# A quarter of the weights' low parts computed on GpSimd instead of VectorE, in one stage of a two-block network

## The chip, the cores and the metric

The kernel runs on one core of one Trainium2 chip. The metric is the device time of one execution in microseconds (us). The kernel before took 2920.99 us (median of 3 runs, 2920.43 to 2922.79).

## The reference

Two residual blocks are applied to one sequence of 256 tokens with 2048 channels, all in fp32. The first block mixes a gated linear recurrence, an attention with forget gates and a pooling branch, and ends with a feed-forward layer. The second block, in which the change lies, is:

```python
h = rms_norm_2(x, attn_norm_w[l])
proj = h @ w_cat
p_rwkv = proj[..., :N_RWKV_IN]
p_gdn = proj[..., N_RWKV_IN:N_IN]
...
y_a, v_first = rwkv7_mixer(p_rwkv, ...)
y_b = gdn_mixer(p_gdn, ...)
y = jnp.concatenate([y_a, y_b], axis=-1).astype(x.dtype)
x = x + y @ w_out[l]
h = rms_norm_2(x, ffn_norm_w[l])
x = x + (jax.nn.silu(h @ ffn_w_gate[l]) * (h @ ffn_w_up[l])) @ ffn_w_down[l]
```

`rwkv7_mixer` shifts each projection by one token, then runs a recurrence over 16 heads of 64 channels. `gdn_mixer` runs a causal convolution of width 4 over tokens, then a gated delta rule over 8 heads of 128 channels.

## The kernel before

Channels lie on the 128 partitions, tokens on the free axis (S = 256). Every large product is `out[128, 256] = sum over k of W_k^T x_k`, with weight tiles of 128 x 128. fp32 accuracy is kept with a split: `weights` (L302) loads a **piece** of up to eight weight tiles (128 x 1024) into `raw` by a DMA of SP's queue, ScalarE (`self.A`) rounds it to `hi` (L314) and VectorE (`self.V`) computes the low part `lo = raw - hi` (L315, by the helper at L206). The activations are split in the same way and stand as 512 columns, 256 high and 256 low. `step3` then issues two matmuls for each k: `hi` against the 512 columns, `lo` against the first 256. `product` (L319) is the loop over the pieces; a product of 2048 rows has two pieces, that is 32 matmuls. `raw` has four buffers, `hi` and `lo` three each. A result in PSUM is completed by `join` (ScalarE copies one half, VectorE adds the other) and `scaled` (a multiply on VectorE).

The stage that the change touches is `mixers` (L898): 51 products of `w2` in four groups, each with an RWKV part (`rwkv_front`, two slots of three products) and a GDN part (`gdn_front`, six products), and `out2_first`, 16 products of `wo2` with 12 tiles (a piece of eight and a piece of four). Between the products stands much small work: `shifted` (L959) and `gdn_front` (L1270) write the scaled projection into a tile whose first columns are zeroed; `rwkv_rest` (L1005) builds decays and chunk matrices `ab`; `diagonals` sends the 16 x 16 diagonal blocks of `ab` through DRAM (`scr`, `d`), inverts them in a chain of 30 small VectorE instructions (`etmp`, `e`), and sends the result back through DRAM (`scs`, `cmp`); `merged_inverse` builds from `cmp` the inverse of the whole chunk, level by level: transposes on TensorE, a copy to `xn` on ScalarE, matmuls with the masked part `off`, a step to `m`, matmuls, an update of `xt` on VectorE, and again. For a GDN group one such inverse serves the group, for an RWKV group there are two.

The order of the instructions on each engine is made by the scheduler of the Tile layer from priorities (`tc.high_priority`, with `ahead_mix = (139, 145)` for the weights in this stage) and from its own costs of the instructions; each engine then runs its list in order and waits on semaphores. `self.parted` marks the stage; the zero columns are written by GpSimd (`self.G.memset` at L962, L1011, L1280), which has no other work in this stage but one more memset.

Of the kernel before, what the change touches and what calls it, by code (L numbers as in the profile page):

```python
# [7 lines left out]
F32 = mybir.dt.float32  # L8
# [7 lines left out]
P = 128  # L16
# [166 lines left out]
class Prog:  # L183
# [83 lines left out]
    pieces = (4, 4, 4, 4)  # L267
    early = []
    parted = False
    narrow = nar3 = nar4 = False  # L270
    nar1 = nar2 = nar5 = True
    turn = 0
# [29 lines left out]
    def weights(self, src, nkt):  # L302

        parts = []
        ahead = self.ahead_mix if self.parted else (self.ahead[self.narrow],) * 2
        for k in range(0, nkt, 8):
            n = min(8, nkt - k) * P
            with self.tc.high_priority(offset=ahead[0]):
                raw = self.rawp.tile([P, n], F32, name="raw", tag="raw")
                self.nc.sync.dma_start(out=raw, in_=src[:, k * P:k * P + n])  # L310
            with self.tc.high_priority(offset=ahead[1]):
                hi = self.hip.tile([P, n], F32R, name="hi", tag="hi")
                lo = self.lop.tile([P, n], F32R, name="lo", tag="lo")
                self.A.copy(hi, raw)  # L314
                self.sub(lo, raw, hi.bitcast(F32))  # L315
            parts.append((k, n // P, hi, lo))
        return parts

# [476 lines left out]
class Block2(Block1):  # L795
# [25 lines left out]
    def block2(self):  # L821
        rh = lambda k, h=self.h: h[:, k]
        with ExitStack() as st:
            self.yp = self.pool("y2", 1, st=st)
            self.y = self.moving(self.yp, 8, "y", at=self.AT["y"])
            self.yg = [None] * 8
            with ExitStack() as st2:
                self.mixers(rh, st2)
            xst = ExitStack()
            self.x = self.pool("xres", 1, st=xst, side="right").tile([P, KT, S], F32, name="xres", tag="xres")  # L830
            self.narrow = self.nar5
            self.out2_second()
        self.narrow = False
        with xst:
            self.ffn("wg2", "wd2", 1e-5, self.feed_out, "left")
            self.last_norm()
# [61 lines left out]
    def mixers(self, rh, st):  # L898
        w2 = self.a["w2"]
        self.tp = self.pool("mx", 3, st=st)  # L900
        self.kp = kp = self.pool("mxk", 1, st=st)
        self.gp = self.pool("mxg", 1, st=st)
        self.parted = True
        self.narrow = self.nar3
        ps = self.product([(w2[0], KT)], rh)
        self.norm2_end()
        self.omu = kp.tile([P, 27], F32, name="omu")
        self.ts(self.omu, self.p("mu_rkv", 0, 27), -1.0, 1.0, ALU.mult, ALU.add)
        self.nka = kp.tile([P, 8], F32, name="nka")
        self.ts(self.nka, self.p("k_a", 0, 8), -1.0)  # L910
        self.wa = kp.tile([P, S], F32, name="wa")
        self.shifted(ps, self.wa, 24)
        self.act(self.wa[:64], self.wa[:64], AF.Tanh)
        self.gd = kp.tile([P, S], F32, name="gd")
        self.shifted(self.product([(w2[1], KT)], rh), self.gd, 25)
        self.mx = kp.tile([P, S], F32, name="mxt")
        self.shifted(self.product([(w2[2], KT)], rh), self.mx, 26)
        self.act(self.gd, self.gd, AF.Sigmoid)
        self.act(self.mx[64:], self.mx[64:], AF.Sigmoid)
        self.sigmoids()  # L920
        self.gdn_gates()
        pend = []
        for g in range(4):
            slots = self.rwkv_group(g, rh, w2)
            front = [self.rwkv_front(2 * g + j, j, rh, w2, slots) for j in range(2)]
            self.step(pend)
            pend.append((slots, front, g, True))
            self.step(pend, first=True)
            slots = self.gdn_group(g)
            front = [self.gdn_front(g, rh, w2, slots)]  # L930
            self.step(pend)
            pend.append((slots, front, g, False))
            self.step(pend, first=True)
        self.narrow = self.nar4
        self.out2_first()
        self.step(pend)
# [22 lines left out]
    def shifted(self, ps, o, j):  # L959

        t = self.w(S + 1, "shf")
        self.G.memset(t[:, 0:1], 0.0)  # L962
        self.scaled(ps, t[:, 1:])
        self.act(o, t[:, 1:], AF.Copy, scale=self.omu[:, j:j + 1])
        self.stt(o, t[:, :S], self.p("mu_rkv", j), o, ALU.mult, ALU.add)
# [39 lines left out]
    def rwkv_rest(self, j, slot, t, slots):  # L1005
# [2 lines left out]

        ch = lambda z: z.rearrange("p (c t) -> p c t", c=2)
        cw, e1, e2 = (ch(self.w(2 * (P + 1), n)) for n in ("cw", "e1", "e2"))  # L1010
        self.G.memset(cw[:, :, 0:1], 0.0)  # L1011
        for c in range(2):
            x = sg[:, c * P:(c + 1) * P]
            self.V.tensor_tensor_scan(out=cw[:, c, 1:], data0=self.c("ones"), data1=x, initial=0.0, op0=ALU.mult, op1=ALU.add)
# [52 lines left out]
        m = self.c("atmask")  # L1067
# [202 lines left out]
    def gdn_front(self, i, rh, w2, slots):  # L1270
        gp = self.gp

        big = gp.tile([P, 6, S], F32, name="gbig", tag="gbig")
        for b in range(6):
            ps = self.product([(w2[27 + 6 * i + b], KT)], rh)
            if b >= 4:
                self.scaled(ps, big[:, b])
                continue
            t = self.w(S + 3, f"gc{b}")
            self.G.memset(t[:, :3], 0.0)  # L1280
            self.scaled(ps, t[:, 3:])
            ch = (i, 4 + i, 8 + 2 * i, 9 + 2 * i)[b]
            o = big[:, b]
            self.act(o, t[:, :S], AF.Copy, scale=self.p("gconv", ch))
            for k in range(1, 4):
                self.stt(o, t[:, k:k + S], self.p("gconv", 16 * k + ch), o, ALU.mult, ALU.add)
        with self.tc.high_priority(offset=self.front_ahead):
            return self.gdn_rest(i, big, slots)
# [147 lines left out]
```

## Time and profile before

| | |
|---|---|
| median of 3 runs | 2920.99 us |
| the profiled execution: its own time / its span | 2924.65 us / 2922.9 us |
| TensorE matmul busy (PE) | 2888.2 us, 99% |
| TensorE weight load (PEld) | 2540.8 us, 87% |
| VectorE (DVE) | 1990.9 us, 68% |
| ScalarE (ACT) | 1506.3 us, 52% |
| GpSimd (POOL) | 21.5 us, 1%, 88 instructions |
| DMA | 515.78 MB, mean 176 GB/s |

Busy time is the union of an engine's instructions, the span is from the first to the last instruction. Matmuls are pipelined, so a busy PE need not be at its peak. The mixers and `out2_first` together lie at about 1571 to 2147 us of the span.

### The profile page before, as it was taken

The page shows a single profiled execution, that of the slowest core. Times are in us where ns is not written, and L with a number is a line of the kernel's source. Part 1 is how long each engine was busy: PE and PEld are TensorE (multiplying, and loading weights), DVE is VectorE, ACT ScalarE, POOL GpSimd, SP SyncE. Part 2 cuts the span into 40 slices and gives each one's busy share as a digit, 9 for nine tenths or more (in the row PEclk, how much of TensorE's full clock was granted, in tenths as well). Part 3 has the DMA queues.
Part 4 walks back from the last instruction along what each step waited for, and adds up shares of the span by engine and source line. Part 5 has one row for each costly group of instructions (what it writes and reads, how often), then busy time and mean ns, then how long its engine had stood idle before and what let it go on. Part 6 is the DMA issues. An engine that isn't in the chain of part 4 may idle for free. (4 is left out here: it accounts for less than half of the span.)

```text
span 2922.9 us, 46401 instructions
## 1 busy us (share of the span) xinstructions
PE 2888.2 (99%) x17676; PEld 2540.8 (87%) x17676; DVE 1990.9 (68%) x3393; ACT 1506.3 (52%) x2448; POOL 21.5 (1%) x88
## 2 busy tenths in 40 slices
PE   8999999999999999999999999999999999999998
PEld 8999988888888888888888878887888888888887
DVE  7855766666766665666667878888776665566665
ACT  6644454444554444444556555666564444444454
POOL 0000000000000000000000000000010000000000
PEclk9999999999999999999999999999999999999999
DMA  6544555555655556555565423233465555655554
GB/s 232 183 160 154 173 188 191 190 188 189 231 190 189 189 177 192 201 191 191 180 206 186 148 87 122 92 130 110 145 207 189 190 186 182 201 191 190 184 177 159
DMA packets 178047, 515.78 MB, mean 176 GB/s; under 512 B 32024, under 2 KB 59040, under 8 KB 177568
## 3 DMA queue, kind: packets, MB, share of 16 engines
q1 hardware_dynamic: 177536, 511.80, 51.9%
q8 instruction: 138, 2.26, 0.3%
q10 hardware_dynamic: 288, 1.02, 0.1%
q14 instruction: 85, 0.70, 0.1%
HBM read 505.66 MB, written 7.09 MB: 175 GB/s over the span
## 5 line engine op out<-in xcount | busy, mean ns | idle before, releaser
L233 PE MATMUL ps<-h,hi 128*128 128x512 f32 (+1 forms) x5904 | 1801.0, 366 | 1.2 <-DVE xp L206 0.9
L206 DVE TENSOR_TENSOR lo<-raw,hi 128x1024 fp32r<-128x1024 f32 (+2 forms) x1028 | 1156.6, 1125 | 759.0 <-ACT hi L314 754.9
L314 ACT CAST hi<-raw 128x1024 fp32r<-128x1024 f32 (+2 forms) x1028 | 997.2, 971 | 1193.3 <-issue 663.8
L233 PE MATMUL ps<-h,lo 128*128 128x256 f32 x5152 | 1410.6, 282 | 0.9 <-DVE lo L206 0.6
L233 PEld LDWEIGHTS ps<-h,hi 128*128 128x128 f32 x5904 | 1041.6, 188 | 164.4 <-issue 6.0
L233 PEld LDWEIGHTS ps<-h,lo 128*128 128x128 f32 x5152 | 969.5, 188 | 29.4 <-issue 2.4
L233 PE MATMUL ps<-mid,hi 128*128 128x512 f32 (+1 forms) x1452 | 486.2, 385 | 0.0
L233 PE MATMUL ps<-mid,lo 128*128 128x256 f32 x1408 | 386.1, 281 | 0.0
L233 PEld LDWEIGHTS ps<-mid,hi 128*128 128x128 f32 x1452 | 265.4, 188 | 50.5
L233 PEld LDWEIGHTS ps<-mid,lo 128*128 128x128 f32 x1408 | 265.1, 188 | 5.3
L206 DVE TENSOR_TENSOR t<-ps,s 128x256 f32<-128x256 f32 x323 | 134.8, 417 | 0.0
L381 ACT COPY s<-ps 128x256 f32<-128x256 f32 x323 | 118.3, 367 | 0.0
L233 PE MATMUL ps<-merged,hi 128*128 128x512 f32 x256 | 88.0, 392 | 0.0
L233 PE MATMUL ps<-merged,lo 128*128 128x256 f32 x256 | 69.0, 280 | 0.0
L233 PEld LDWEIGHTS ps<-merged,hi 128*128 128x128 f32 x256 | 47.0, 188 | 9.6 <-DVE merged L206 0.2
L233 PE MATMUL ps<-y,hi 128*128 128x512 f32 (+1 forms) x160 | 49.3, 359 | 1.7 <-ACT hi L314 1.4
L233 PEld LDWEIGHTS ps<-merged,lo 128*128 128x128 f32 x256 | 48.1, 188 | 1.3
L233 PE MATMUL ps<-yg,hi 128*128 128x512 f32 (+1 forms) x160 | 48.6, 354 | 0.0
L233 PE MATMUL ps<-yb,hi 128*128 128x512 f32 x128 | 46.1, 393 | 0.0
L233 PE MATMUL ps<-yc,hi 128*128 128x512 f32 x128 | 46.1, 393 | 0.0
L233 PE MATMUL ps<-ya,hi 128*128 128x512 f32 x128 | 45.9, 391 | 0.0
L206 DVE TENSOR_TENSOR t<-ps,xres 128x256 f32<-128x256 f32 x78 | 33.1, 424 | 12.9 <-PE ps L233 7.0
(383 smaller groups left out, 2307.8 us busy)
## 6 DMA issues: line engine op xcount, KB each, us to landing
raw<-wg SPq DMA_DIRECT2D x352, 512.0 KB, 4.2
raw<-w SPq DMA_DIRECT2D x292, 512.0 KB, 3.6
raw<-wd SPq DMA_DIRECT2D x128, 512.0 KB, 3.5
raw<-wbr SPq DMA_DIRECT2D x48, 512.0 KB, 3.5
raw<-wo SPq DMA_DIRECT2D x48, 512.0 KB, 4.3
raw<-wd SPq DMA_DIRECT2D x128, 192.0 KB, 3.1
raw<-wo SPq DMA_DIRECT2D x32, 256.0 KB, 3.2
xin<-x SPq DMA_DIRECT2D x4, 512.0 KB, 6.4
```

What stands on the lines that cost most here:

```text
L206: return (e or self.V).tensor_tensor(out=o, in0=x, in1=y, op=op)
L233: return self.T.matmul(o, lhsT=l, rhs=r, start=start, stop=stop, skip_group_check=True)
L314: self.A.copy(hi, raw)
L381: self.A.copy(s[:rows], ps[:rows, S:])
```

## The change

In the stage, a piece of more than 512 columns has its `lo` computed in two parts: VectorE takes the first three quarters (768 of 1024 columns), GpSimd the last quarter (256 columns). A flag `shared` is set where `parted` is set and cleared ahead of the last feed-forward layer. The pieces of 512 columns in `out2_first` and `out2_second` stay whole. The memsets of the zero columns in `shifted`, `rwkv_rest` and `gdn_front` move from GpSimd to VectorE.

```diff
@@ class Prog
+    shared = False
...
@@ weights
                 self.A.copy(hi, raw)
-                self.sub(lo, raw, hi.bitcast(F32))
+                m = n - 2 * P if self.shared and n > 4 * P else n
+                self.sub(lo[:, :m], raw[:, :m], hi[:, :m].bitcast(F32))
+                if m < n:
+                    self.sub(lo[:, m:], raw[:, m:], hi[:, m:].bitcast(F32), self.G)
...
@@ block2
-        self.narrow = False
+        self.narrow = self.shared = False
...
@@ mixers
-        self.parted = True
+        self.parted = self.shared = True
...
@@ shifted
-        self.G.memset(t[:, 0:1], 0.0)
+        self.V.memset(t[:, 0:1], 0.0)
...
@@ rwkv_rest
-        self.G.memset(cw[:, :, 0:1], 0.0)
+        self.V.memset(cw[:, :, 0:1], 0.0)
...
@@ gdn_front
-            self.G.memset(t[:, :3], 0.0)
+            self.V.memset(t[:, :3], 0.0)
```

The scheduler makes a new order for the whole stage. Line numbers of the changed kernel are larger by 1 to 4.

**Order 1.** GpSimd's whole list from the pooling branch on (`pu`, `gtr` are memsets that stay). First the first rows of it before, which go on in the same pattern, then all of it now:

```order
L682 MEMSET pu 128x2x16
L962 MEMSET shf 128x1 x6
L1011 MEMSET cw 128x2
L962 MEMSET shf 128x1 x3
L1011 MEMSET cw 128x2
L1280 MEMSET gc_16870 128x3
L1280 MEMSET gc_16926 128x3
```

```order
L1250 MEMSET gtr 128x256
L686 MEMSET pu 128x2x16
L206 ISA
L206 TENSOR_TENSOR lo<-raw,hi 128x256 x118
L206 TENSOR_TENSOR acc_22557<-acc_22557,q 128x256 x15
```

The 51 memsets of the stage are gone from GpSimd's list, and 118 subtractions stand in it: 102 pieces of the 51 products and the 16 pieces of eight tiles in `out2_first`. The 15 instructions on `acc` are those of `out2_second`, there before and after.

**Order 2.** SP's queue at the first RWKV group's way through DRAM (`raw` is a weight piece, `scs` the inverted diagonals going out, `cmp` the same coming back), before and now:

```order
L310 DMA raw<-w 128x1024
L1107 DMA d<-scr_16775 64x256
L310 DMA raw<-w 128x1024 x4
L1122 DMA scs_16819<-e 64x256
L310 DMA raw<-w 128x1024
L1124 DMA cmp<-scs_16819 128x8x16
L310 DMA raw<-w 128x1024 x3
```

```order
L311 DMA raw<-w 128x1024
L1111 DMA d<-scr_16793 64x256
L311 DMA raw<-w 128x1024 x5
L1126 DMA scs_16837<-e 64x256
L1128 DMA cmp<-scs_16837 128x8x16
L311 DMA raw<-w 128x1024 x3
```

Ahead of `scs` as many pieces are loaded as before (one fewer stands further up), and no piece is loaded any more between `scs` and `cmp`.

**Order 3.** TensorE's list at the inverse of the second GDN group, from its first transposes (`pb<-cst,xt`) on, before and now (`ps` rows are the large products, `pf` rows belong to the front of the next RWKV slot, `pb` rows to the inverse):

```order
L236 MATMUL pb<-cst,xt 128x128 x4
L233 MATMUL ps<-h,hi 128x512
L233 MATMUL ps<-h,lo 128x256
L233 MATMUL ps<-h,hi 128x512
L233 MATMUL ps<-h,lo 128x256
L233 MATMUL ps<-h,hi 128x512
L233 MATMUL pb<-xn,off 128x128 x4
L233 MATMUL ps<-h,lo 128x256
L233 MATMUL ps<-h,hi 128x512
L233 MATMUL pf<-tok,ak 128x64
```

```order
L236 MATMUL pb<-cst,xt 128x128 x4
L236 MATMUL pf<-cst,bt 128x128
L236 MATMUL pf<-cst,kt 128x128
L236 MATMUL pf<-cst,r_18910 128x128 x2
L233 MATMUL pf<-ar_19110,bt 128x256
L233 MATMUL pb<-xn,off 128x128 x4
L233 MATMUL pf<-ar_19110,bt 128x256
L233 MATMUL pf<-ar_19110,kt 128x256
L233 MATMUL pb<-xt,m_19456 128x128 x4
L233 MATMUL pf<-ar_19110,kt 128x256
L233 MATMUL pf<-ar_19111,bt 128x256 x2
L1167 MATMUL pb<-cst,xt 128x128 x4
```

Before, the steps of the inverse stood among large products: 13 of their matmuls from the first transposes to the second, 16 from there to the third. Now none stands there up to the second and 3 up to the third; work of the RWKV front lies between instead. The third GDN group's inverse has the same pattern, with 13 and 16 before and 4 and none now.

## Rows read from the trace of the kernel before

**Rows 1.** The page's first line.
```profile
span 2922.9 us, 46401 instructions
```
**Rows 2.** Stretches: us; busy (instructions) of PE, PEld, DVE, ACT, POOL; PEclk, DMA, GB/s.
```profile
1571.00:2147.00 576.00, 566.16 (x3524) 469.59 (x3523) 451.38 (x1103) 345.34 (x684) 5.25 (x48) 1.00 0.38 124
1780.00:1800.00 20.00, 20.00 (x117) 17.60 (x116) 18.05 (x51) 11.34 (x14) 0.00 (x0) 1.00 0.56 191
2020.00:2040.00 20.00, 20.00 (x117) 17.58 (x117) 18.56 (x55) 10.76 (x14) 0.00 (x0) 1.00 0.48 156
1684.00:1688.00 4.00, 1.73 (x7) 1.64 (x8) 2.48 (x5) 0.97 (x3) 0.00 (x0) 0.74 0.32 117
1688.00:1692.00 4.00, 4.00 (x28) 3.67 (x26) 2.65 (x6) 0.59 (x3) 0.10 (x1) 0.83 0.38 131
```
**Rows 3.** TensorE's longest waits, 1571 to 2147: us in total, times, longest.
```profile
PE pb L236 <- DVE xt L206: 3.5, 4, 2.8
PE ps L233 <- DVE lo L206: 1.7, 1, 1.7
```
**Rows 4.** VectorE's groups by shape, 1571 to 2147: busy us, mean ns | idle before.
```profile
L206 DVE TENSOR_TENSOR lo<-raw,hi 128x1024 fp32r<-128x1024 f32 x112 | 136.5, 1220 | 33.3 <-ACT hi L314 33.1
L206 DVE TENSOR_TENSOR lo<-raw,hi 128x512 fp32r<-128x512 f32 x21 | 14.4, 687 | 6.3 <-ACT hi L314 5.5 <-PE ps L233 0.3
...
L1016 DVE COPY mid<-cw 128x2 f32<-128x2 f32 x8 | 1.3, 164 | 0.1
```
**Rows 5.** GpSimd's largest group of memsets in the stage, same columns.
```profile
L962 POOL MEMSET shf<- 128x1 f32 x27 | 2.8, 110 | 1550.9 <-PE pf L233 1096.2 <-PE ps L233 424.3 <-DVE rs_w L206 14.2
```
**Rows 6.** Tile view of acc, GpSimd, 2140 to 2180: ns min/median/max.
```profile
L206 POOL TENSOR_TENSOR acc<-acc,q x15: 728/860/1685, 2147.6 to 2176.9; 128x256 f32<-128x256 f32 x15
```
**Rows 7.** Tile view of h, VectorE, 1400 to 1570, with GpSimd idle: same columns.
```profile
L218 DVE SCALAR_TENSOR_TENSOR h<-xres,gfa,h x16: 476/479/480, 1445.7 to 1563.8; 128x256 fp32r<-128x256 f32 x16
```
**Rows 8.** VectorE's groups by shape, 2145 to 2177, while GpSimd works on acc.
```profile
L218 DVE SCALAR_TENSOR_TENSOR h<-xres,par,h 128x256 fp32r<-128x256 f32 x15 | 10.5, 710 | 0.1
L206 DVE TENSOR_TENSOR lo<-raw,hi 128x512 fp32r<-128x512 f32 x13 | 9.7, 742 | 3.0 <-ACT hi L314 2.7
```
**Rows 9.** Timeline, 2157 to 2163: start, us, engine, instruction.
```profile
2160.22 1.89 POOL L206 TENSOR_TENSOR acc<-acc,q 128x256 f32<-128x256 f32 x2 [0.49 <-ACT q L230]
2160.26 1.24 DVE L206 TENSOR_TENSOR lo<-raw,hi 128x512 fp32r<-128x512 f32 x1
...
2161.43 0.96 DVE L218 SCALAR_TENSOR_TENSOR h<-xres,par,h 128x256 fp32r<-128x256 f32 x1
```
**Rows 10.** Timeline, 1677 to 1687: the first RWKV group's way through DRAM.
```profile
1677.47 0.47 SPq L1122 DMA_DIRECT2D scs<-e  x1
...
1678.61 0.33 SPq L310 DMA_DIRECT2D raw<-w  x1
...
1679.41 0.38 SPq L1124 DMA_DIRECT2D cmp<-scs  x1
...
1685.52 1.29 DVE L206 TENSOR_TENSOR xt<-cmp,cst 128x512 f32<-128x512 f32 x2 [3.08 <-DMA cmp<-scs]
...
1686.27 1.11 PE L236 MATMUL pb<-cst,xt 128*128 128x128 f32 x4 [2.84 <-DVE xt L206]
```
**Rows 11.** Tile view of cmp: from issue to landing, eight transfers.
```profile
DMA to landing us min/median/max: 1.8/2.4/6.1
```
**Rows 12.** Timeline, 1856 to 1863: the second GDN group's inverse, first level.
```profile
1856.36 0.66 PE L236 MATMUL pb<-cst,xt 128*128 128x128 f32 x4 [0.22 <-DVE xt L206]
...
1857.18 0.56 ACT L1139 COPY xn<-pb 128x512 f32<-128x512 f32 x1
...
1857.80 1.16 PE L233 MATMUL pb<-xn,off 128*128 128x128 f32 x8
...
1861.08 0.69 DVE L206 TENSOR_TENSOR xt<-pb,xt 128x512 f32<-128x512 f32 x1 [0.37 <-PE pb L233]
...
1862.42 0.60 PE L1163 MATMUL pb<-cst,xt 128*128 128x128 f32 x4
```

## The prediction

> **What bounds the kernel now.** I read the page first, then the stretch of the mixers by windows, then TensorE's waits in it, and last the timeline at the places where it waits. The profiled execution took 2924.65 us, with a span of 2922.9 [rows 1]; it lies 3.7 us above the median of the runs, 2920.99. The sum below is a difference within the profiled execution, and I add it to the median.
>
> In the stage that changes, 1571 to 2147, TensorE is busy for 566.16 of 576 us [rows 2]. What it stands idle there, 9.84 us, is nearly all that any edit of the other engines can win. To this comes some time at the lower clock: in 1684 to 1692 the granted clock was on average 0.74 and then 0.83 of the upper of its two levels (2.4 GHz; the lower is 1.2) [rows 2], right behind TensorE's longest wait [rows 3], and that costs 4 x 0.26 + 4 x 0.17 = 1.7 us. So the ceiling of a gain is 11.5 us, 0.4%. VectorE is busy for 451.38 us, 78%, but unevenly: where the six products of a GDN front follow each other TensorE runs without a gap, 117 matmuls in 20 us or 0.171 us each, and VectorE is at 18.05 to 18.56 of 20 us [rows 2]. For `lo` TensorE waited once, 1.7 us; its largest wait is for `xt`, the start of an inverse [rows 3]. A quicker `lo` as such thus frees little.
>
> The 0.2% by which I part faster from slower is 5.8 us, about what a measurement of this kernel tells from no change.
>
> **The subtraction on VectorE.** A `lo` of 1024 columns takes 1.220 us, one of 512 columns 0.687 [rows 4]. For 768 I take the middle, 0.954. The 118 pieces save 118 x 0.266 = 31.4 us of VectorE's time.
>
> **The subtraction on GpSimd.** The only two-input work of GpSimd in the trace, on 128x256 as here, took 728 ns at the least, 860 in the median, 1685 at the most [rows 6]. Its result is needed late: it holds the seventh and eighth weight tile, and TensorE has six pairs of matmuls before, 12 x 0.171 = 2.05 us. So TensorE waits for it only if it comes over 2 us behind VectorE's part, and I cost that at nothing; its cover is the lead of three `lo` buffers, and without that 1.685 us would still be less than 2.05. The release of `hi` and `raw`, for which ScalarE and SP's queue now also wait on GpSimd, is late by as much at the most; a ring of four pieces lasts 4 x 16 x 0.171 = 10.9 us, so this is hidden too.
>
> **What it costs VectorE that GpSimd runs.** While GpSimd works on `acc`, the same instruction on `h` takes 710 ns instead of 479, and a `lo` of 512 columns 742 instead of 687 [rows 4, 7, 8]. Over 15 instructions of GpSimd that is 15 x 0.231 + 13 x 0.055 = 4.2 us, 0.28 each. The single cases are larger: a `lo` that began 0.04 us behind GpSimd took 1.24 us instead of 0.69, and the `h` behind it, with the next `acc` waiting, 0.96 instead of 0.48 [rows 9]. So the loss c of VectorE per piece lies between 0.28 and 0.55 us. In the mixers GpSimd and VectorE are released by the same cast, so the single case must be common, but the mean says that many of the 15 found nothing to slow; I take the middle, c = 0.40, or 47 us in all, with 33 and 65 as the ends.
>
> **The Trainium skill on this.** Its page "SBUF — State Buffer", section "Who interferes with whom", says that a VectorE instruction with two inputs in SBUF contends with a GpSimd instruction that reads SBUF, and that the later one fully blocks until the first has ended. Rows 9 agree for the single case; the mean of 0.28 is well below a full block. By the rule at its word c would be GpSimd's whole 0.73 us, and the sum would be that of the second case below, at its upper end of 2936 us, in place of 2925.
>
> **The memsets.** 51 leave GpSimd, where one takes 110 ns [rows 5]; VectorE's nearest row is a copy of two columns, 164 ns [rows 4]. That is 5.6 to 8.4 us of VectorE's time, 7 taken. What is queued behind one is the multiply into the same tile, which waits for the same buffer, so no wait is added.
>
> VectorE's sum is -31.4 + 47 + 7 = +23 us, 474 of 576 (ends 458 and 494). In the dense stretches a window holds 117 / 16 = 7.3 pieces: 18.05 to 18.56, plus 7.3 x (0.40 - 0.266) = 1.0, plus 0.2 for memsets, is 19.3 to 19.8 of 20. It still fits, barely. Some of this reaches TensorE as short waits: +1 us (0 to +4). The wait for `lo` of 1.7 us gets shorter: -1 us (-1.7 to 0).
>
> **What the new order moves.** First, the way through DRAM of the first RWKV group (order 2). Before, a weight piece of 512 KB was issued at 1678.61 between `scs` and `cmp`; `cmp` was issued at 1679.41 and VectorE got it at 1685.5, and TensorE stood for 2.84 us [rows 10]. That is 6.1 us to land, where the median is 2.4 [rows 11]. With the piece behind `cmp`, up to 3.7 us are won. But TensorE's list has these transposes one piece earlier, 16 x 0.171 = 2.7 us, while the chain on VectorE ends at the same piece. Net -3.7 + 2.7 = -1 us; ends are +2.7, nothing won, and -4.5, wait and low clock both gone.
>
> Second, the inverses of the second and third GDN group (order 3). Before, the first level took 6.06 us from transposes to transposes, 1856.36 to 1862.42 [rows 12], with 13 large matmuls, 2.2 us, inside. The chain alone needs 0.66 + 0.56 + 1.16 + a second set of matmuls like the first, of which 0.4 us lies behind the last `m`, + the tail of `m`, about 0.6, + 0.69 for `xt`: about 4.1 us, an estimate from these rows, of which TensorE works 0.66 + 1.16 + 1.16 = 3.0. It would idle 1.1 us a level; the front's matmuls that now stand there cover that if their own inputs are ready, and these come from the same VectorE list, which has `ab`, `ak` and `xt` in turn. I take 2 us for each of the two groups (0 to 3), +4 in all. The large matmuls that stood there run elsewhere at full speed; they win nothing back.
>
> Third, at the second and third RWKV group TensorE comes to the first transposes 20 and 5 matmuls earlier, the chain on VectorE ends one piece (16) and none earlier: 4 and 5 matmuls less cover, 0.7 and 0.9 us. +1 us (0 to +1.6).
>
> **The sum.** +1 - 1 - 1 + 4 + 1 = +4 us: 2920.99 + 4 = **2925 us**. The ends add up to -6 and +14.
>
> **The rivals.** *VectorE becomes the bound (slower).* If c is above 0.44 to 0.51 us, 7.3 pieces bring the dense stretches over 20 us. At 0.55 they are at 20.4 to 21.0, 2 to 5% too long; four GDN fronts of 12 pieces are 4 x 12 x 16 x 0.171 = 131 us, so +4.6; at GpSimd's whole 0.73 it is 8%, +11. With +4 for the order this gives 2929.6 to 2936, say 2932. For it speaks that both single cases, 0.48 and 0.55, lie at or above the point; against it the mean of 0.28 and the idle time of VectorE ahead of `lo`, 33 us [rows 4], which a backlog would fill first.
>
> *The gain shows (faster).* The first group's wait and its low clock go (-4.5), the wait for `lo` goes (-1.7), and the RWKV front covers the two inverses in full: 2914.8. For it speaks the 6.1 us landing that the new queue avoids; against it that three things must all come true, and that the transposes stand earlier.
>
> That the subtraction does not move is out: 118 rows of it stand in GpSimd's list (order 1).
>
> **The numbers.** The forecast, within 5.8 us of before, has 0.49, the bound on VectorE 0.37, the gain 0.14. The second case is the larger tail, so the range reaches from 2917 to 2938: below lies part of the gain alone, above it a block worse than GpSimd's own time. The likeliest case's own range is 2917 to 2927. Faster 0.14, same 0.49, slower 0.37.
>
> **What would show it.** `lo` of 768 columns near 0.95 us where GpSimd is idle and near 1.5 where it began first; GpSimd busy for 118 x 0.73 to 1.0 us, some 90 to 120 more; VectorE near 474 us in the stage. TensorE's wait at the first RWKV group near 2 us, with `cmp` landing in under 3; new waits on `xt`, `m` or `ab` inside the second and third GDN inverse of some 2 us each. In the dense stretches TensorE still at 117 matmuls per 20 us; if it has fewer there and waits for `lo`, the slower rival is right. I am wrong in kind if TensorE waits for GpSimd at the seventh tile, or if the stage's idle time falls under 6 us.

## The result and the profile after

The changed kernel takes 2961.29 us (median of four runs, 2956.92 to 2964.22) against 2920.71 for the kernel before on the same chip: 40.6 us slower, ratio 1.0137, 95% interval 1.0124 to 1.0149. The forecast was 2925, the range 2917 to 2938. The result lies above it, and above the rival in which VectorE becomes the bound.

The stage of the mixers, by windows (columns as in [rows 2]): the whole of it, a dense stretch, the stretch behind that, and 2 x 4 us of this one.

```profile
1571.00:2187.00 616.00, 581.77 (x3530) 479.96 (x3529) 461.99 (x1151) 344.27 (x683) 132.44 (x113) 0.98 0.36 116
1771.00:1791.00 20.00, 20.00 (x122) 17.46 (x122) 17.20 (x42) 9.07 (x14) 7.33 (x6) 1.00 0.44 139
1791.00:1811.00 20.00, 15.89 (x84) 13.24 (x83) 13.67 (x35) 10.59 (x12) 3.36 (x4) 0.94 0.52 164
1804.00:1808.00 4.00, 0.88 (x5) 0.49 (x3) 1.44 (x3) 1.35 (x2) 0.00 (x0) 1.00 0.69 191
1808.00:1812.00 4.00, 3.54 (x14) 3.26 (x15) 1.83 (x3) 2.11 (x4) 0.78 (x1) 0.57 0.27 93
```

The stage is 40 us longer than in [rows 2]. TensorE is idle for 616 - 581.77 = 34.2 us of it in place of 9.8, which is 24.4 of the 40. The other 15.6 us are busy time for the same matmuls. Most of that is the clock: its mean is 0.98 of the upper level, 0.02 x 616 = 12 us, where [rows 2] had 1.00. The last two rows show one case: from 1804 TensorE stands for most of 4 us, and right behind that the granted clock is 0.57 on average over 4 us, mostly the lower of its two levels. The stage has eight waits of over 2 us. Behind seven of them stands such a stretch; behind the one of 2.41 us at the first RWKV group, from 1685 to 1693, the granted clock stayed at 1.00.

VectorE is busy for 461.99 us in 616. It has not become the bound as a whole: this dense stretch still has 122 matmuls in 20 us without a gap, and VectorE is busy for 17.20 us there.

TensorE's waits, 1571 to 2187 (columns as in [rows 3]):

```profile
PE pb L236 <- DVE xt L206: 10.0, 3, 4.0
PE pf L233 <- DVE kp L218: 8.2, 4, 2.8
PE ps L233 <- DVE lo L206: 3.9, 5, 2.8
PE pb L1167 <- DVE xt L206: 3.9, 3, 3.6
PE pf L236 <- ACT gtr L230: 2.4, 1, 2.4
...
PE pf L233 <- DMA up<-up: 0.2, 1, 0.2
```

In [rows 3] there were 3.5 us for `xt` and none for `kp` among the longest. TensorE nowhere waits for GpSimd. It waits for VectorE at the end of two chains of small steps: `kp`, which a group's RWKV front hands to TensorE, and `xt`, with which an inverse begins, behind the chain on the diagonal blocks and the way through DRAM. The row of L1167 is almost all one wait of 3.63 us, for the `xt` between the first two levels of the inverse in the last GDN group; before, TensorE had no wait of over 0.1 us there.

VectorE's and GpSimd's groups by shape in the stage (columns as in [rows 4]), two of them before and then now:

```profile
L218 DVE SCALAR_TENSOR_TENSOR gbig<-gc,par,gbig 128x256 f32<-128x256 f32 x48 | 22.2, 479 | 0.4
...
L218 DVE SCALAR_TENSOR_TENSOR gout<-gout,par,rs_y 128x256 f32<-128x256 f32 x8 | 3.8, 480 | 0.1
```

```profile
L206 DVE TENSOR_TENSOR lo<-raw,hi 128x768 fp32r<-128x768 f32 x111 | 112.0, 1011 | 37.0 <-ACT hi L315 34.7 <-PE ps L233 1.2 <-issue 0.2
L218 DVE SCALAR_TENSOR_TENSOR gbig<-gc,par,gbig 128x256 f32<-128x256 f32 x48 | 25.4, 549 | 3.1 <-ACT gbig L230 2.8
L206 DVE TENSOR_TENSOR t<-ps,s 128x256 f32<-128x256 f32 x50 | 20.4, 409 | 0.1
L218 DVE SCALAR_TENSOR_TENSOR gout<-gout,par,rs_y 128x256 f32<-128x256 f32 x8 | 5.8, 721 | 0.1
...
L966 DVE MEMSET shf<- 128x1 f32 x24 | 1.4, 59 | 0.1
...
L206 POOL TENSOR_TENSOR lo<-raw,hi 128x256 fp32r<-128x256 f32 x112 | 133.6, 1193 | 472.6 <-ACT hi L315 380.0 <-DVE gbig L218 22.9 <-PE ps L233 20.7
```

A `gbig` took 479 ns in the mean and takes 549, a `gout` took 480 and takes 721. Those have both inputs in SBUF. `t`, which reads one input from PSUM, took 414 and takes 409. This agrees with the Trainium skill, "SBUF — State Buffer", section "Who interferes with whom": a VectorE instruction with two inputs in SBUF contends with a GpSimd instruction that reads SBUF, one with at most one SBUF input (outside the two-port modes) does not.

What a held-up step looks like, in the timeline of VectorE (start, us, engine, instruction) in the diagonal chain ahead of the longest wait, and TensorE at its end:

```profile
1784.23 0.71 DVE L206 TENSOR_TENSOR etmp<-d,e 64x15 f32<-64x15 f32 x1 [0.93 <-DMA d<-scr]
1784.97 0.18 DVE L206 TENSOR_TENSOR e<-e,etmp 64x15 f32<-64x15 f32 x1
...
1787.62 0.74 DVE L206 TENSOR_TENSOR e<-e,etmp 64x48 f32<-64x48 f32 x1
...
1790.16 0.75 DVE L206 TENSOR_TENSOR e<-e,etmp 64x60 f32<-64x60 f32 x1
...
1807.71 1.29 DVE L206 TENSOR_TENSOR xt<-cmp,cst 128x512 f32<-128x512 f32 x2 [1.54 <-DMA cmp<-scs]
...
1804.48 0.40 PE L233 MATMUL ps<-h,hi 128*128 128x512 f32 x1
1808.46 1.11 PE L236 MATMUL pb<-cst,xt 128*128 128x128 f32 x4 [3.58 <-DVE xt L206]
```

A step of 0.18 to 0.21 us takes 0.71 to 0.75 where a subtraction of GpSimd was under way (begun at 1784.17, 1787.35 and 1789.73); each of the three steps ends 0.04 to 0.07 us behind that subtraction. In this chain, 1784 to 1801, six of thirty steps are hit.

To measure how much VectorE is held up, I took every VectorE instruction of the stage that lasted over 0.06 us longer than the median of its own kind in a run whose GpSimd reads nothing (e3 below), and added up the excess: 87 instructions, 39.9 us. Over 118 pieces that is 0.34 us a piece; the prediction had taken 0.40.

### The profile page after: what moved, and what is told of

Its sections match the earlier page's. It is cut to its first block, busy times and chain, and to the rows that moved or that the text cites. A ratio compares the mean times of both kernels' runs of the same rounds, so it can differ in the third digit from the quotient of the medians.

```text
span 2960.2 us, 46630 instructions
## 1 busy us (share of the span) xinstructions
PE 2902.0 (98%) x17676; PEld 2550.1 (86%) x17676; DVE 2001.8 (68%) x3444; ACT 1505.3 (51%) x2448; POOL 158.1 (5%) x155
## 4 chain that ended last, share of the span: by engine, by line
PE 89%; DVE 6%; DMA 2%; ACT 2%; issue 2%; POOL 0%; SPq 0%; ACTq 0%; POOLq 0%; DVEq 0%
PE ps L233 81%; PE pb L233 5%; PE pf L233 3%; DVE lo L206 2%; ACT hi L315 1%; DVE e L206 0%; DVE etmp L206 0%; DVE gbig L218 0%; PE pf L236 0%; DMA xo<-xs 0%; PE pb L1167 0%; DMA scs<-e 0%; DMA cmp<-scs 0%; PE pb L236 0%; DMA par<-par 0%
## 5 line engine op out<-in xcount | busy, mean ns | idle before, releaser
L206 DVE TENSOR_TENSOR lo<-raw,hi 128x1024 fp32r<-128x1024 f32 (+3 forms) x1028 | 1132.1, 1102 | 765.7 <-ACT hi L315 758.9
L206 POOL TENSOR_TENSOR lo<-raw,hi 128x256 fp32r<-128x256 f32 x118 | 142.0, 1204 | 1722.5 <-ACT hi L315 1629.9
```

Of the source, the lines that this page charges most:

```text
L206: return (e or self.V).tensor_tensor(out=o, in0=x, in1=y, op=op)
```

## The experiments

Two things came with the change: GpSimd reads while VectorE works, and all four other engines have a new order. To part them, I pinned orders: the program is traced, the scheduler's order of another version is taken, and each instruction of TensorE, VectorE, ScalarE and SP is queued behind its neighbour in that order. "Old order" is that of the kernel before, "new order" that of the changed kernel. GpSimd has only the low parts and, in all runs below, the zero columns (in the changed kernel VectorE has them); it is not pinned. The edits below are shortened to the lines that matter, with simplified names.

```diff
+    # order[engine]: places in program order, as the scheduler put them in the other version
+    for e, l in lists.items():
+        seq = [l[k] for k in order[e]]
+        for x, y in zip(seq, seq[1:]):
+            tc.add_manual_dep(y, x.name, NO_SYNC, reason="order")
```

### The quarter in the old order, and the new order without it (e1, e2)

e1 is the changed `weights` with the old order and the zero columns on GpSimd. e2 is the kernel before (`m = n` in `weights`) in the new order.

> GpSimd takes the quarter, but TensorE, VectorE, ScalarE and SP keep the order that they had before (every instruction is queued behind its neighbour of before); the zero columns stay on GpSimd. Two theories. Order: nearly all of the 40.6 us come from the new order that the scheduler made, because it puts first transposes, ar and kp on TensorE's list closer behind the VectorE chains that feed them. Then this run takes 2917 to 2927 us, the idle time of TensorE in the mixers stays at 8 to 15 us, and there are one or two stretches at half clock. Contention: the 40.6 us come from GpSimd, whose reads hold up VectorE's instructions with two inputs, and the order only moves where it shows. Then this run takes 2945 to 2965 us with the same places waiting on xt, kp and lo. If ScalarE's waits for GpSimd (26 us in all after the change) were what counts, this run would be slow as well, with casts waiting for lo by GpSimd.

> The other half of the pair: VectorE computes the whole low part as before, GpSimd has nothing but the zero columns, and the four engines run in the order of the changed kernel. Order: 2945 to 2970 us; VectorE has 31 us more of its own subtraction and about 25 us less of held-up instructions, so the waits of TensorE at the first transposes (xt) and at kp, and the half-clock stretches behind them, stand where the changed kernel has them. Contention: 2918 to 2926 us, and no more than two stretches at half clock.

e1 took 2939.07 us (before 2924.31; ratio 1.0049, 1.0034 to 1.0064), e2 2941.7 (1.0058, 1.0043 to 1.0073). Both lie between what the two theories said: neither the order nor GpSimd alone makes the 40.6 us. TensorE's waits over the whole stage, e1 first, then e2:

```profile
PE pb L237 <- DVE xt L207: 6.2, 5, 3.8
PE ps L234 <- DVE lo L207: 3.4, 4, 1.7
PE pf L234 <- DMA up<-up: 2.5, 4, 1.1
...
PE pf L234 <- DVE kp L219: 1.7, 2, 1.1
```
```profile
PE pb L237 <- DVE xt L207: 9.0, 3, 3.7
PE pb L1185 <- DVE xt L207: 3.7, 3, 3.4
PE pf L234 <- DVE kp L219: 3.6, 4, 1.3
```

`xt` and `kp` are among the places in both. In e2 no VectorE instruction of the stage is held up (counted as above), and yet the waits are there; with 31 us less of `lo` on VectorE in the same order (e3 below) `kp` falls from 3.6 to 0.4 us and the first `xt` row from 9.0 to 4.9. e1 also waits 2.5 us for `up`, a load on SP's queue. Neither the kernel before nor e9 has such a wait, and in e1 SP's weight loads wait 28.4 us in all for GpSimd to give `raw` back. So the late release, which the prediction held to be hidden, very likely shows in the old order; e5 below has such waits with nobody held up.

### GpSimd writes but doesn't read (e3, e9)

```diff
-                    self.sub(lo[:, m:], raw[:, m:], hi[:, m:].bitcast(F32), self.G)
+                    self.G.memset(lo[:, m:].bitcast(F32), 0.0)
```

> The order of the changed kernel; VectorE subtracts three quarters, and GpSimd fills the last quarter of the low part with zeros in place of subtracting (that quarter of the weights' low parts is left out of the result). GpSimd then reads nothing, VectorE is 31 us lighter than before. Order: still 2940 to 2960 us, at most 15 us under the changed kernel, since the lists are the same. Contention: back to 2914 to 2926 us. What lies between this run and the changed kernel is the price of GpSimd's reads and of the longer wait for it in this order; what lies between this run and the kernel before is the order's own.

> The order of before on TensorE, VectorE, ScalarE and SP, VectorE subtracts three quarters, GpSimd fills the last quarter with zeros (left out of the result) and reads nothing. It closes the square: with the quarter subtracted the old order took 2939 (before 2924 on that chip), the new order 2927 with the fill. If VectorE's 31 us were worth anything to TensorE where the order has room, this run takes 2914 to 2919 us; if, as I predicted, a lighter low part frees little, 2920 to 2925. The waits of TensorE at kp and xt should be those of before, shorter by at most 1 us each, and the price of the held-up steps in the old order is then what lies between this run and 2939: 14 to 20 us.

In the new order the fill took 2926.89 us (before 2924.31; 1.0014, 1.0004 to 1.0023), in the old order 2916.51 (before 2923.23; 0.9979, 0.9969 to 0.9988). The order theory had 2940 to 2960 for e3 and fails; contention had 2914 to 2926 and is missed by 0.9 us, since some of the order's cost is left. e9 is in the range of "worth something", against my prediction. The chain's steps stay whole, here in the tile view of `etmp` in e3 and then in the changed kernel (ns min/median/max):

```profile
L207 DVE TENSOR_TENSOR etmp<-d,e x120: 151/196/220, 1660.4 to 2084.0; 64x15 f32<-64x15 f32 x8, 64x28 f32<-64x28 f32 x8, 64x39 f32<-64x39 f32 x8, 64x48 f32<-64x48 f32 x8
```
```profile
L206 DVE TENSOR_TENSOR etmp<-d,e x120: 152/198/757, 1668.2 to 2118.2; 64x15 f32<-64x15 f32 x8, 64x28 f32<-64x28 f32 x8, 64x39 f32<-64x39 f32 x8, 64x48 f32<-64x48 f32 x8
```

e3 and the changed kernel have the same list on TensorE, so they can be laid side by side. In e3 the same wait stands so:

```profile
1794.62 0.39 PE L234 MATMUL ps<-h,hi 128*128 128x512 f32 x1
1796.29 0.66 PE L237 MATMUL pb<-cst,xt 128*128 128x128 f32 x4 [1.27 <-DVE xt L207]
```

The changed kernel starts the first of these 1804.48 - 1794.62 = 9.86 us later and the second 12.17 us later: 2.3 us are lost in this wait, and 1.6 more by 1812 at the lower clock. Laid side by side in this way over the whole stage, the loss comes at some ten such places (`gtr`, `kp`, `xt`, the first product of `out2_first`), by 1 to 2.6 us in the step itself and up to 5 with the clock. Between them the two run at nearly the same pace.

### The square

| us against before, on the same chip | VectorE whole | VectorE ¾, GpSimd fills | VectorE ¾, GpSimd subtracts |
|---|---|---|---|
| old order | 0 | -6.7 (e9) | +14.8 (e1) |
| new order | +17.4 (e2) | +2.6 (e3) | +39.1 (e10) |

Each has an interval of some 3 to 5 us to both sides. 31 us less for VectorE are worth 6.7 us in the old order and 17.4 - 2.6 = 14.8 in the new. GpSimd's subtracting in place of filling costs 14.8 + 6.7 = 21.5 us in the old order, 39.1 - 2.6 = 36.5 in the new. The new order costs 17.4, 9.3 or 24.3 us by the column. So both count, and each makes the other dearer.

### Only the quarter, and the zero columns (e4, e10)

e4 is the change without the zero columns, the scheduler free, which gives a third order. e10 has the new order pinned and only the memsets back on GpSimd. In both:

```diff
-        self.V.memset(t[:, 0:1], 0.0)
+        self.G.memset(t[:, 0:1], 0.0)
...
-        self.V.memset(cw[:, :, 0:1], 0.0)
+        self.G.memset(cw[:, :, 0:1], 0.0)
...
-            self.V.memset(t[:, :3], 0.0)
+            self.G.memset(t[:, :3], 0.0)
```

> Only the quarter on GpSimd, the zero columns stay there as well, and the scheduler is free; it makes a third order that differs from both. Order: the time is that of this order, 2930 to 2965 us, with the waits at other places than in the changed kernel. Contention: 2950 to 2962, as the changed kernel less the few us that 51 memsets of 0.06 to 0.16 us cost VectorE, with waits at the same kind of place. If the memsets on VectorE were the cause, 2918 to 2926.

> The changed kernel with its order, but the 51 memsets of the zero columns back on GpSimd. As predicted the memsets are 5.6 to 8.4 us of VectorE's time beside other work, so 0 to 4 us faster than the changed kernel: 2957 to 2965 with before at 2924. If the memsets themselves stood in the chains that TensorE waits for, 8 us or more faster: under 2955. On GpSimd each memset waits for a product in a buffer that is not free yet, and the subtractions are queued behind it, so slower than the changed kernel is possible too (2967 to 2975).

e4 took 2960.19 us (before 2924.31; ratio 1.0120, 1.0104 to 1.0135), e10 2962.32 (before 2923.23; 1.0137, 1.0120 to 1.0154). The memsets make no difference that can be measured. Since e10 is otherwise the changed kernel with its own order pinned, pinning and memsets together make no difference to be seen in the new order; for the old order there is no such run. e4 does not part the theories, since it lies in the range of both; it shows that the change is costly in either order that the scheduler made for it.

### Late or held up (e5, e6)

Reading in place of filling does two things: it holds VectorE up, and GpSimd gives `hi` and `raw` back later, for which ScalarE's casts wait 24.3 us in the changed kernel. e5 keeps the second, e6 the first.

```diff
+            # e5: late, hardly any reading
+            one = lambda k: self.sub(lo[:, k:k + 1], raw[:, k:k + 1], hi[:, k:k + 1].bitcast(F32), self.G)
+            one(m); [self.G.memset(lo[:, m + 1:n - 1].bitcast(F32), 0.0) for _ in range(3)]; one(n - 1)
...
+            # e6: reads constants, gives raw and hi back at once
+            self.sub(lo[:, m:m + 1], raw[:, m:m + 1], hi[:, m:m + 1].bitcast(F32), self.G)
+            self.sub(lo[:, m + 1:], z, z, self.G)
```

> The order of the changed kernel. GpSimd fills the last quarter with zeros three times over (3 x 0.31 us as the fill took in the run before), between two subtractions of a single column that make it wait for the cast and give hi and raw back only at the end: GpSimd is about as long and as late as in the changed kernel (1.19 us a piece there), but reads next to nothing (the last quarter of the low parts is left out, but for two columns). Held up: the 36 us between the fill alone (2927) and the changed kernel come from VectorE's steps that wait while GpSimd reads, so this run takes 2924 to 2934 us and the small steps of the diagonal chain stay at 0.19 us. Late: they come from the late release of hi and raw and from ScalarE's 26 us of waiting for GpSimd, so this run takes 2945 to 2965 us.

> The mirror image, in the same order: GpSimd subtracts one column of raw and hi (which gives them back at once) and then, over the other 255 columns of the quarter, a piece of the constants from itself, which reads as much as the real subtraction and writes zeros (the last quarter of the low parts is left out, but for one column). Held up: 2950 to 2967 us, the chain's steps at up to 0.75 us as in the changed kernel. Late: 2925 to 2938 us.

Both took the same: 2945.42 us (before 2923.71; 1.0078, 1.0061 to 1.0095) and 2945.27 (1.0077, 1.0062 to 1.0092). By the time alone e5 speaks for lateness and e6 for neither. The waits tell them apart, e3 first, then e5 and e6:

```profile
PE pb L237 <- DVE xt L207: 4.9, 3, 2.2
PE pb L1185 <- DVE xt L207: 2.7, 3, 2.4
...
PE pf L234 <- DVE kp L219: 0.4, 1, 0.4
```
```profile
PE pf L234 <- DMA up<-up: 9.0, 4, 4.4
PE pb L237 <- DVE xt L207: 4.8, 3, 1.8
PE pb L1184 <- DVE xt L207: 4.3, 3, 4.0
...
PE pf L234 <- DVE kp L219: 0.4, 1, 0.4
```
```profile
PE pb L237 <- DVE xt L207: 9.2, 3, 3.4
PE pf L234 <- DVE kp L219: 4.2, 5, 1.8
...
PE pb L1185 <- DVE xt L207: 2.7, 3, 2.4
...
PE pf L234 <- DMA up<-up: 1.3, 1, 1.3
```

In e5 TensorE waits for `up`, a load on SP's queue behind weight loads that wait for `raw`. The changed kernel has 0.2 us of that, so most of this loss is e5's own: GpSimd was later there than I had meant it to be, since a one-column subtraction took 0.53 us in the mean, and a piece 1.9 us in place of 1.2. At `xt` and `kp` e5 waits nearly as e3 does (`kp` 0.4 us in both, `xt` of the transposes 4.8 and 4.9), though ScalarE's casts wait for GpSimd by 12.6 + 9.1 = 21.7 us there: lateness does not cost at these places. There is one exception: between the levels of the last GDN inverse (L1184 here, L1167 in the changed kernel) e5 waits 4.3 us and the changed kernel 3.9, but e3 and e6 2.7. That points to lateness for the 1.2 us that the changed kernel loses there. e6 waits at the places of the changed kernel, at the first `xt` row nearly as long (9.2 us against 10.0), at `kp` half as long (4.2 against 8.2). Its held-up time, counted as above, is 22.7 us in place of 39.9, and its loss against e3 is 19 us in place of 36.5. By the ratio of held-up time one would expect 21, which is within the noise of 19.

### Which pieces (e7, e8)

The new order; GpSimd subtracts in the pieces of a list and fills in the others.

```diff
+        if self.piece in self.some:  # e7: 43 pieces ahead of the ten places; e8: the other 75
+            self.sub(lo[:, m:], raw[:, m:], hi[:, m:].bitcast(F32), self.G)
+        else:
+            self.G.memset(lo[:, m:].bitcast(F32), 0.0)
```

> The order of the changed kernel; GpSimd subtracts only in 43 of the 118 pieces, those whose subtraction lay in the 9 to 20 us ahead of the ten places at which TensorE lost most against the run with the fill (the starts of inverses, kp, gtr, and the first product of the last stage), and fills zeros in the other 75 (whose last quarter of the low parts is left out). If what counts is a chain of small VectorE steps that ends just ahead of TensorE, this run loses most of the 36 us: 2948 to 2962. If what counts is VectorE's throughput, it loses 43/118 of them: 2938 to 2944.

> The complement: GpSimd subtracts in the other 75 pieces and fills in the 43. Chains: 2926 to 2938 us. Throughput: 75/118 of 36 us, 2947 to 2953.

e7 took 2948.68 us (before 2923.71; 1.0085, 1.0070 to 1.0100), e8 2938.68 (1.0056, 1.0041 to 1.0071). Against e3 that is +22.4 and +12.4 us: 0.52 us for each of the 43 pieces and 0.17 for each of the 75. VectorE was held up by 18.7 us in e7 and 22.6 in e8 (e8's profiled execution took 2944.26 us, 5.6 above its median). Where it happens counts for more than how much, as the chains say, but both runs lie at the throughput end of the chains' range, e8 0.7 us past it: the far pieces are not free.

### Aimed at the harmless pieces, and one input (e11, e12)

e11 is the attempt at a version that pays: the old order, the quarter subtracted by GpSimd in 59 pieces, the other 59 whole on VectorE. e12 is e9 with a multiply in place of the fill.

```diff
-                m = n - 2 * P if self.shared and n > 4 * P else n
+                m = n - 2 * P if self.shared and n > 4 * P and piece in self.some else n  # e11
...
-                    self.G.memset(lo[:, m:].bitcast(F32), 0.0)
+                    self.ts(lo[:, m:], raw[:, m:], 0.0, e=self.G)  # e12
```

> Could the division pay where it is aimed? The order of before; GpSimd subtracts the quarter only in 59 of the 118 pieces, those whose subtraction did not lie in the 9 to 23 us ahead of a place at which TensorE waited in the run of the quarter in the old order; VectorE computes the other 59 whole. The fill run (2916.5) says that 31 us less of VectorE's own work are worth 6.7 us to TensorE in this order, so half of them at most 3.4. In the run of the quarter in the old order these 59 pieces had about half of the held-up VectorE instructions too, each by about 0.5 us, mostly in gbig, r, lo and sc and few in the diagonal chain. If only held-up steps just ahead of TensorE cost: 2919 to 2924 us. If every held-up step costs alike: 2927 to 2932. Against before at 2924 it would then be a gain of 0 to 0.15%, or a loss of 0.1 to 0.3%.

> What of GpSimd's instruction holds VectorE up: in the order of before GpSimd multiplies the quarter of raw by zero into lo (one input in place of two; the last quarter of the low parts is left out) as soon as raw is there. If one input read by GpSimd is enough to hold VectorE's two-input instructions up, some 60 to 90 of them are longer by 0.3 to 0.5 us again and the run takes 2928 to 2941 us; if it takes two inputs on both sides, none is, and the run takes 2915 to 2921 like the fill.

e11 took 2928.02 us (before 2924.08; 1.0015, 1.0006 to 1.0024), slower than before. It is in the range of "every held-up step costs alike": only two of its held-up steps lie in the diagonal chain, 0.9 of 18.4 us, and it still lost. A likely reason, argued and not shown, is that a step that waits in VectorE's list also puts off all that stands behind it there, until the list is next idle; how much of the loss is the later release of `hi` and `raw` was not parted. None of the versions run here that compute the whole result beats the kernel before; e9 and e12 are faster, but leave a quarter of the low parts out.

e12 took 2919.11 (0.9987, 0.9978 to 0.9996): 5.0 us under the kernel before, where e9 was 6.7 under, a difference within the noise. The time is in the range of the second case, the holds are those of neither: 54 instructions of the stage are held up, but only by 9.5 us in all, since the longest hold is short (`etmp` again, e12):

```profile
L207 DVE TENSOR_TENSOR etmp<-d,e x120: 151/200/466, 1663.9 to 2082.9; 64x15 f32<-64x15 f32 x8, 64x28 f32<-64x28 f32 x8, 64x39 f32<-64x39 f32 x8, 64x48 f32<-64x48 f32 x8
```

## Why the prediction was wrong

**The subtraction on VectorE.** Right: 768 columns take 0.958 us in the median, as against 0.954, and up to 1.50 when GpSimd began first.

**GpSimd's part, costed at nothing on TensorE.** Right in that TensorE never waits for it in the changed kernel. Its own time was undersized: 1.19 us in the mean in place of 0.73 to 1.0. That the late release of `hi` and `raw` is hidden holds there but for some 1.2 us at the last GDN inverse, and very likely not in the old order, where e1 waits 2.5 us for `up`.

**The loss of VectorE.** Right in size: 0.34 us a piece in place of 0.40, 39.9 us in place of 47. The Trainium skill's rule of a full block ("SBUF — State Buffer", "Who interferes with whom") nearly holds for the instruction that is hit by a subtraction: 0.75 us in place of 0.2, with an end just behind GpSimd's, and no hold is over 0.6 us. It does not hold for the multiply of e12, which takes 0.85 us at the least and holds a step up by 0.27 at the most. There were 87 held-up instructions for 118 pieces, so its word is not the mean.

**The memsets.** Mis-sized and harmless: 59 ns in place of 110 to 164, since a copy of two columns was not a near enough row.

**The dense stretches.** Right: they stayed full, and VectorE did not become the bound there. The rival that I gave 0.37 had the sign and not the mechanism. (Its dense stretch at 0.55 comes to 20.3 to 20.8 us by its own terms, not 20.4 to 21.0, which changes nothing.)

**"Some of this reaches TensorE as short waits: +1 us (0 to +4)."** This is the step that failed. I had set VectorE's sum of +23 us against its idle time and found room for it. But VectorE's idle time is room for throughput, and what TensorE waits for at `kp` and `xt` is the end of a chain: there a step that is held up by 0.55 us, or a `gout` that stands in the list ahead of the chain, comes out whole where the consumer stands close behind. With the old order the change was forecast at +1 - 1 = 0 us, and e1 measured +14.8. e1 against e9 puts the price of GpSimd's subtracting at 21.5 us in the old order, e10 against e3 at 36.5 in the new, late release included. The same error hid the gain: 31 us less of `lo` is worth 6.7 us in the old order, where I had put 1 us.

**The new order, +4 us in all.** Mis-sized: 9.3 to 24.3 us in the square. The first RWKV group went as thought in one part: `cmp` now lands within 3.3 us at the worst, not 6.1, and the wait is 2.41 us, not 2.84 (in e10, with the same order, it is 3.65). At the inverses of the second and third GDN group the gaps that the trace shows add up to some 0.1 and 0.5 us, less than the 2 each that I took; the one long wait inside a GDN inverse, 3.63 us, is in the fourth group, which I did not look at. What was far too small is the third term, "4 and 5 matmuls less cover", 1 us: at these two RWKV groups TensorE now waits 3.58 and 4.01 us, and 1.27 and 1.44 of that stand in e3 too, with nobody held up.

And I did not look at `kp` at all. TensorE waits for it in four of the eight slots now. At these four it came 0.15, 0.15, 0.42 and 0.42 us behind VectorE's last step before, so the trace of before already showed that there was hardly any cover. The third of them in the timelines of before and of e3, VectorE's last step and TensorE's first:

```profile
1882.37 0.48 DVE L218 SCALAR_TENSOR_TENSOR kp<-r,par,kp 128x256 f32<-128x256 f32 x1
...
1883.27 0.59 PE L233 MATMUL pf<-kp,cst 128*128 128x256 f32 x2
```
```profile
1886.26 0.48 DVE L219 SCALAR_TENSOR_TENSOR kp<-r,par,kp 128x256 f32<-128x256 f32 x1
...
1886.79 0.70 PE L234 MATMUL pf<-kp,cst 128*128 128x256 f32 x2 [0.38 <-DVE kp L219]
```

Before, TensorE comes 0.42 us behind VectorE and doesn't wait; in the new order, with nobody held up, it waits 0.38. In the changed kernel it waits 2.82 us, and VectorE's list shows why (the same slot, 1899 to 1905):

```profile
1899.46 0.96 DVE L218 SCALAR_TENSOR_TENSOR gout<-gout,par,rs_y 128x256 f32<-128x256 f32 x1
...
1900.55 0.96 DVE L206 TENSOR_TENSOR gout<-gout,gbig 128x256 f32<-128x256 f32 x1
...
1903.51 0.94 DVE L206 TENSOR_TENSOR bt<-bt,e 128x256 f32<-128x256 f32 x1
1904.38 0.47 DVE L218 SCALAR_TENSOR_TENSOR kp<-r,par,kp 128x256 f32<-128x256 f32 x1
...
1904.90 1.22 PE L233 MATMUL pf<-kp,cst 128*128 128x256 f32 x2 [2.82 <-DVE kp L218]
```

Three held-up steps, 0.5 us each, stand ahead of `kp`, and two of them are not of its chain. Against e3 they make 1.6 of the 2.4 us that the wait has grown; the other 0.9 VectorE had lost by the time of the first row.

**The clock.** I had counted the lower clock as something that a removed wait gives back (1.7 us). I did not count that new waits bring stretches of it along, as seven of the eight waits of over 2 us did here; that made 12 of the 40 us.

## What to carry to other kernels

Where VectorE feeds chains to a bound TensorE, cost a change of VectorE at the consumers that stand close behind it: for each, look up how far TensorE is behind now and in the new order, and count what of the delay goes beyond that. A share of GpSimd in work with two SBUF inputs gave VectorE 0.27 us a piece and took 0.34, before any of it reached TensorE. And a new order from a scheduler is a change of its own: pin the old one with the new work, and the new one with the old work, before explaining either.

## What had not been expected of the hardware

- A GpSimd multiply of one SBUF input, 128x256, held VectorE's steps up by at most 0.47 - 0.20 = 0.27 us, though it took 0.97 itself in the mean. A subtraction of two inputs, 0.72 us at the least, held them up by 0.55.
- Filling 128x256 with zeros on GpSimd took 0.31 us and held nothing up: `lo` of 768 columns stayed at 0.953 in the mean.
- A GpSimd subtraction of one column took 0.53 us in the mean beside VectorE's work, more than the fill of 254 columns (0.31).
